# Convolution, LayerNorm sums, q/k norms and scores re-arranged in one step of a hybrid attention and convolution encoder

## The chip, the cores and the metric

The kernel runs on one core of one Trainium2 chip. TensorE (PE) multiplies matrices; VectorE (DVE), ScalarE (ACT) and GpSimd (POOL) do elementwise work; SyncE (SP) issues DMAs. PSUM is the memory into which TensorE accumulates, SBUF the working memory, HBM the memory outside. The metric is the device time of one launch in microseconds (us), smaller being better. Every engine takes its instructions in a fixed order.

## The reference

One layer for 1024 prompt frames and 32 sample frames of 1024 channels, 16 heads of 64. Cut to what matters:

```python
h = rmsnorm(x, norm_g)
q = rmsnorm(cols(OFF_Q), q_g) * HEAD_DIM ** -0.5      # per head
k = rmsnorm(cols(OFF_K), k_g)                         # cols(a) = h @ w_in[:, a:a + w]
v = cols(OFF_V);  logf = log_sigmoid(cols(OFF_F) + b_f)
u = cols(OFF_UA) * sigmoid(cols(OFF_UB))
ga, gb, ma, mb = cols(...), ...
s = einsum('bqhd,bkhd->bhqk', q, k) + C[t] - C[s]     # C = cumsum(logf), causal
o = softmax(s) @ v
conv = causal_dwconv(u_ext, w_dw) + b_dw              # width 31, per channel
ya = (o * silu(ga)) @ w_pa
yb = (silu(layernorm(conv, ln_g, ln_b)) * silu(gb)) @ w_pb
y = x + (sigmoid(ma) * ya + sigmoid(mb) * yb) @ w_out
```

The 32 sample frames attend to 512 cached keys besides their own, and their convolution starts from 30 cached rows. q, k, v, log f and the last rows of u are outputs too. Everything is float32 with a small tolerance, so a product is built of three: each operand is split into a high part of reduced precision and the rest, and TensorE multiplies high by high, rest by high and high by rest.

## The kernel before, in words

Prompt and sample stand side by side as 1056 columns. A projection of 128 output channels (`steps`, L102) takes 24 matmuls for each of three chunks of 352 columns; each chunk is accumulated in one PSUM bank and then evacuated. Its weights are loaded as `raw`, cast to the high part `wh` by ScalarE (L85) and split into the rest `wl` by GpSimd (L88). In the first half of the program five PSUM banks are handed round for such chunks.

The stages, in program order:

1. **Input.** A run of idle matmuls (L253), then tokens are normalised (`x_norm`), transposed by TensorE and split (`x_split`), in four column chunks; the first convolution input u0 (from the groups "ub" and "ua") is projected along with them, with a sigmoid for each chunk.
2. **u1 and v.** `u_proj(1)` makes the next 128 channels of u. Then v is projected token-major in four column groups of 260 (256 of v, 4 of f), nine row tiles each (eight prompt tiles of 128 rows and one sample tile of 32). u2 stands between the second and the third group.
3. **log f, q and k.** The log-sigmoid is computed by an exp and a series of short DVE operations at high priority (L408 to L423). Then 8 times "k" and "q": each chunk is squared by ScalarE, split, summed over the 64 channels of a head by TensorE (`bones`, L476 and L477), and turned into 1/root by a Sqrt on ScalarE (L479) and a reciprocal on VectorE (L480); L481 multiplies. u3 stands at f = 3.
4. **Gates ga**, with u4, u5, u6 between them.
5. **Attention.** 16 heads of 8 query blocks. A block's `scores` go into one of two PSUM buffers `psS`; VectorE takes the maximum (L659), ScalarE the exp (L661) into one of three buffers `P`, VectorE 1/sum (L663), GpSimd scales (L664). `turn` transposes P on TensorE (L681) and splits it (L685, L686); `values` multiplies by v (L697, L698). Between the parts of a block, `fill(4)` runs four steps of three matmuls of an unrelated projection: u7 and 21 gate tiles. The sample's four groups of heads stand among the blocks.
6. **Last stage.** The 3 gate tiles left over, then the projections "pa", "pb" and "out", with `ln_out` making the convolution branch's input beside "pa".

The convolution is done by VectorE: per 128 channels 30 `tap`s (L168), each a multiply-add over 1086 columns, after a first tap on ScalarE (L166). The taps of u(f) are put into a list, and `pump` takes some of them out between the pieces of other work, from stage 2 into the attention. The finished y(f) is added to `mean` (L172, L174) and stored. LayerNorm then works inside the attention: mean over channels by TensorE, y loaded again, mean subtracted (L742), stored, squared, squares summed by GpSimd (L747), 1/root (L756, L757), y loaded a third time, multiplied (L763) and stored.

What sets the order: a scheduler lays out every engine's instructions at build time by its own estimate of times and by priorities (evacuations stand high, taps low); only TensorE's order in the attention is as written. On the chip an engine waits at the head of its order whatever stands behind it.

## Time and profile before

| | |
|---|---|
| time, median of 3 runs | 1467.45 us (1467.08 to 1468.04) |
| the profiled execution | 1474.0 us, its span 1472.2 us |
| mean granted TensorE clock | 0.982 |
| TensorE busy | 1422.8 us, 97% of the span |
| VectorE, ScalarE, GpSimd busy | 943.6, 627.4, 690.8 us |
| DMA | 217.47 MB, 148 GB/s over the span |

TensorE's busy time counts pipelined matmuls, so an engine that is busy all the time may still issue less than it could. It is read together with the number of matmuls in a stretch and the granted clock: a stretch of pure 352-column projections without a stall holds 159 matmuls in 25 us. The profiled execution took 6.55 us more than the median of the runs. By time the stages lie so: input to 54 us, u1 and v to about 214, q and k to about 450, ga to about 616, attention to about 1160, last stage to 1472.

### The profile page before, as it was taken

Reading aid. Unit: us, or ns where it says so; the run is one execution under the profiler, and the core shown is the slowest. Engines: PE = TensorE matmul, PEld = TensorE weight load, DVE = VectorE, ACT = ScalarE, POOL = GpSimd, SP = SyncE. Lnnn points to the kernel's source line nnn. Section 1 sums busy time; section 2 is a strip of 40 time slices with the busy share of each in tenths; the row PEclk is TensorE's granted clock in tenths of the full one; section 3 lists DMA queues with packets and bytes.
Section 4 is the critical chain, followed back from the end, with each engine's and each line's share of the span. In section 5 each row is a group of like instructions: output and inputs, shape, how many; then the busy total and the mean of one; then the engine's idle time right before and its main releaser. Section 6 shows DMA issues by size and latency. Waiting matters only on the chain.

```text
span 1472.2 us, 24868 instructions
## 1 busy us (share of the span) xinstructions
PE 1422.8 (97%) x9465; PEld 1379.1 (94%) x9465; DVE 943.6 (64%) x1194; ACT 627.4 (43%) x1257; POOL 690.8 (47%) x734
## 2 busy tenths in 40 slices
PE   8999898999999999899999999899999999999999
PEld 7899898999999999898899999788999999999998
DVE  5699898849995999979955545765554442132211
ACT  6423124444554222264455555664555486222110
POOL 3488444747885343444534334634332364244321
PEclk9999999999999999999999999999999999999999
DMA  4244233333455522243555456857552597444421
GB/s 172 76 139 153 81 139 114 120 120 106 144 174 165 158 96 90 79 116 103 136 171 148 140 155 189 284 176 258 175 155 69 194 337 265 145 129 155 146 88 50
DMA packets 114935, 217.47 MB, mean 148 GB/s; under 512 B 17856, under 2 KB 75072, under 8 KB 114816
## 3 DMA queue, kind: packets, MB, share of 16 engines
q1 hardware_dynamic: 114384, 215.52, 46.5%
q8 instruction: 75, 1.23, 0.4%
q14 instruction: 44, 0.36, 0.1%
q10 hardware_dynamic: 432, 0.37, 0.1%
HBM read 137.89 MB, written 77.95 MB: 147 GB/s over the span
## 4 chain that ended last, share of the span: by engine, by line
PE 60%; DVE 12%; DMA 3%; ACT 2%; issue 1%; POOL 1%; SPq 0%; DVEq 0%; ACTq 0%
PE pj L96 46%; DVE y L168 10%; PE ptr L681 4%; PE po L697 2%; PE po L698 2%; PE psS L654 2%; PE psS L655 2%; DMA yv<-s_y 1%; DMA V<-s_v 1%; DVE ri L480 1%; DMA s_y<-yv 1%; PE po L605 1%; DVE yv L742 1%; PE psS L657 0%; POOL wl L88 0%
## 5 line engine op out<-in xcount | busy, mean ns | idle before, releaser
L96 PE MATMUL pj<-xh,wh 128*128 128x352 f32 (+2 forms) x1552 | 514.9, 333 | 9.2 <-DVE qn L481 3.2
L96 PE MATMUL pj<-xh,wl 128*128 128x352 f32 (+2 forms) x1552 | 500.4, 323 | 1.1 <-POOL wl L88 1.1
L96 PE MATMUL pj<-xl,wh 128*128 128x352 f32 (+2 forms) x1552 | 499.7, 325 | 0.0
L88 POOL TENSOR_TENSOR wl<-raw,wh 128x384 fp32r<-128x384 f32 (+1 forms) x264 | 306.4, 1190 | 323.2 <-ACT wh L85 318.7
L168 DVE SCALAR_TENSOR_TENSOR y<-u,vec_t,y 128x1086 f32<-128x1086 f32 x240 | 378.6, 1577 | 24.1 <-ACT y L166 14.8
L96 PEld LDWEIGHTS pj<-xh,wh 128*128 128x128 f32 x1552 | 295.7, 191 | 13.4 <-ACT xh L325 4.7
L96 PEld LDWEIGHTS pj<-xh,wl 128*128 128x128 f32 x1552 | 296.7, 191 | 2.3 <-POOL wl L88 2.3
L96 PEld LDWEIGHTS pj<-xl,wh 128*128 128x128 f32 x1552 | 293.6, 191 | 0.3
L664 POOL TENSOR_SCALAR P<-P,nm 128x128 f32<-128x128 f32 (+7 forms) x128 | 111.4, 871 | 234.2 <-DVE nm L663 219.0
L85 ACT CAST wh<-raw 128x1024 fp32r<-128x1024 f32 x88 | 92.2, 1048 | 159.5 <-PE pj L96 123.5
L659 DVE TENSOR_REDUCE nm<-psS 128x1 f32<-128x128 f32 (+7 forms) x128 | 96.4, 753 | 72.3 <-PE psS L657 56.6
L685 ACT CAST pth<-ptr 128x512 fp32r<-128x512 f32 (+1 forms) x192 | 86.9, 481 | 97.7 <-PE ptr L681 96.6
L480 DVE RECIPROCAL ri<-ri 128x352 f32<-128x352 f32 x48 | 112.0, 2339 | 23.4 <-ACT ri L479 23.3
L686 DVE TENSOR_TENSOR ptl<-ptr,pth 128x512 fp32r<-128x512 f32 (+1 forms) x192 | 101.9, 550 | 18.1 <-ACT pth L685 16.0
L661 ACT ACTIVATE P<-psS,nm 128x128 f32<-128x128 f32 (+7 forms) x128 | 95.3, 744 | 39.3 <-DVE nm L659 32.8
L681 PE MATMUL ptr<-ident,P 128*128 128x128 f32 x576 | 86.8, 278 | 14.2 <-POOL P L664 11.5
L382 PE MATMUL pjv<-vwh,xh 128*128 128x260 f32 (+1 forms) x288 | 82.3, 286 | 4.6 <-DVE u L212 4.6
L382 PE MATMUL pjv<-vwl,xh 128*128 128x260 f32 (+1 forms) x288 | 82.2, 285 | 0.0
L382 PE MATMUL pjv<-vwh,xl 128*128 128x260 f32 (+1 forms) x288 | 82.2, 285 | 0.0
L697 PE MATMUL po<-pth,V 128*128 128x256 f32 x320 | 79.3, 284 | 1.7 <-DMA V<-s_v 1.7
L698 PE MATMUL po<-ptl,V 128*128 128x256 f32 x320 | 78.3, 282 | 0.0
L681 PEld LDWEIGHTS ptr<-ident,P 128*128 128x128 f32 x576 | 62.9, 143 | 15.9 <-POOL P L664 12.2
(188 smaller groups left out, 2530.8 us busy)
## 6 DMA issues: line engine op xcount, KB each, us to landing
raw<-wf SPq DMA_DIRECT2D x88, 512.0 KB
yv<-s_y SPq DMA_DIRECT2D x16, 528.0 KB
s_y<-yv SPq DMA_DIRECT2D x16, 528.0 KB
s_v<-vb SPq DMA_DIRECT2D x32, 256.0 KB
QB<-s_q SPq DMA_DIRECT2D x32, 256.0 KB
KB<-s_k SPq DMA_DIRECT2D x32, 256.0 KB
V<-s_v SPq DMA_DIRECT2D x16, 512.0 KB
kT<-qn SPq DMA_DIRECT2D x8, 528.0 KB
```

The lines of the kernel that those rows point to most:

```text
L88: nc.gpsimd.tensor_sub(wl[:, k0:k1, :], raw[:, k0:k1, :], f32(wh[:, k0:k1, :]))
L96: nc.tensor.matmul(ps, a[:, kt, :], b(kt, sl), start=(first and n == 0), stop=(last and n == N - 1))
L168: nc.vector.scalar_tensor_tensor(ys[0], u[:, i:i + CW], w, ys[0], op0=ALU.mult, op1=ALU.add)
L382: nc.tensor.matmul(ps[:r, :VC], a, b, start=(n == 0), stop=(n == 23))
L480: nc.vector.reciprocal(ri, ri)
L659: nc.vector.tensor_reduce(nm[:, 0:1], ps[:, :nb, :w], axis=AX.XY, op=ALU.max, negate=True)
L661: nc.scalar.activation(P[:, :nk].rearrange("p (b w) -> p b w", b=nb), ps[:, :nb, :w], AF.Exp, bias=nm[:, 0:1], accum_out=nm[:, 1:2])
L664: nc.gpsimd.tensor_scalar(P[:, :nk], P[:, :nk], nm[:, 2:3], 1.0, op0=ALU.mult, op1=ALU.mult)
L681: nc.tensor.transpose(pt[:, 128 * j:128 * j + 128], P[:, 128 * (4 * u + j):128 * (4 * u + j) + 128], ident)
L686: nc.vector.tensor_sub(ptl[:, js, qo], p3, f32(pth[:, js, qo]))
L697: nc.tensor.matmul(po[:, :256], V[:, j, :], pth[:, j, :], start=(j == 0), stop=False)
L698: nc.tensor.matmul(po[:, :256], V[:, j, :], ptl[:, j, :], start=False, stop=(j == njb - 1))
```

## The change

**Convolution.** u3 now stands ahead of q and k, u4, u5, u6 at f = 2, 4, 6 and u7 ahead of the ga gates, so all eight convolutions are issued before the attention, and their pool is closed before it. There are two y buffers instead of one. The attention's fills are 22 gate tiles, without u7; 2 gate tiles are left for the last stage, and two blocks of head 8 have no fill.

**LayerNorm.** `conv_done` stores y(f) and then works on it while it lies in SBUF: it subtracts a shift, the mean over the first 128 channels of y(0) (four float32 matmuls, `shift_of`), adds the rest to `mean` (DVE), squares it in place (ACT) and adds the squares to `rstd` (POOL). In the attention only the two sums over channels remain, the variance is their difference, and 1/root is made by Ln and Exp. `ln_out` subtracts the mean and multiplies by 1/root itself (two DVE operations per tile), so y is loaded once and not stored again.

**Norms by log and exp.** In `x_norm` and in q and k the root and its reciprocal become Ln and Exp on ScalarE, from one preloaded table; after each u's sigmoid the table is loaded again. The log-sigmoid moves behind f = 1, without high priority.

**Scores.** Scores are issued three blocks ahead of their turn instead of two; the loads of heads and samples one block earlier. The number of psS and P buffers stays.

**v.** A group's sample tile (24 matmuls) becomes 8 float32 matmuls, four of which write to different 32-row groups of one bank; the four partial sums are added by ScalarE and VectorE.

**Input.** Three column chunks instead of four, some squares on VectorE, u0's sigmoid once at the end, 46 idle matmuls instead of 56.

Three places where the order moved. First VectorE ahead of the evacuation of u2 (its multiplication by the sigmoid, L212 before and L248 now). Before, from the last evacuation of u1:

```order
L168 SCALAR_TENSOR_TENSOR y<-u,vec_t,y 128x1086 x16
L172 COPY mean<-y 128x1024
L172 COPY mean<-y 128x32
L168 SCALAR_TENSOR_TENSOR y<-u,vec_t,y 128x1086 x25
L212 TENSOR_TENSOR u<-pj,u 128x352
```

Now the end of the same piece (taps are L212 here; 6 of them stand ahead of the first row):

```order
L212 SCALAR_TENSOR_TENSOR y<-u,vec_t,y 128x1086 x13
L437 TENSOR_REDUCE vs<-v_1099 32x260
L212 SCALAR_TENSOR_TENSOR y<-u,vec_t,y 128x1086 x2
L438 COPY z<-vs 32x4
L212 SCALAR_TENSOR_TENSOR y<-u,vec_t,y 128x1086 x14
L189 TENSOR_TENSOR y<-y,shift 128x1024
L189 TENSOR_TENSOR y<-y,shift 128x32
L212 SCALAR_TENSOR_TENSOR y<-u,vec_t,y 128x1086
L192 COPY mean<-y 128x1024
L192 COPY mean<-y 128x32
L212 SCALAR_TENSOR_TENSOR y<-u,vec_t,y 128x1086 x7
L248 TENSOR_TENSOR u<-pj,u 128x352
```

From the start of the convolution to u2's evacuation there were 55 taps and are 57 now, and two reductions for the sample's v and the subtraction of the shift have come in.

Second ScalarE where v ends. Before, q and k begin there (L472, L473), behind the exp of the log-sigmoid:

```order
L386 COPY vf<-pjv 32x256
L390 COPY z<-pjv 32x4
L413 ACT_TABLE_LOAD
L413 ACTIVATE ee<-az 128x144
L472 ACTIVATE sqf<-pj 128x352
L473 CAST sqh<-sqf 128x352
```

Now u3 stands there (L241 are the copies of its "ub" chunks), and the exp, the square of a finished convolution (L195) and the cast of k's first weights (L91) stand among them:

```order
L241 COPY u<-pj 128x352
L478 ACT_TABLE_LOAD
L478 ACTIVATE ee<-az 128x144
L241 COPY u<-pj 128x352
L195 ACTIVATE y<-y 128x1086
L241 COPY u<-pj 128x320
L241 COPY u<-pj 128x32
L91 CAST wh<-raw 128x1024
L244 ACT_TABLE_LOAD
L244 ACTIVATE u<-u 128x1024
L244 ACTIVATE u<-u 128x32
L564 ACT_TABLE_LOAD
```

k's first weights now stand behind the square, which itself stands behind VectorE's subtraction and sum.

Third TensorE at the first `turn` of the attention. Before (psS are scores, ptr the transposes, pj the fills):

```order
L96 MATMUL pj<-xl,wh 128x352
L654 MATMUL psS<-KB,QB 128x384
L655 MATMUL psS<-KA,QA 128x384
L657 LDWEIGHTS identb
L657 MATMUL psS<-cmaskb,identb 128x128
L681 MATMUL ptr_6485<-ident,P 128x128
```

Now:

```order
L102 MATMUL pj<-xl,wh 128x352
L731 MATMUL psS<-KB,QB 128x384
L732 MATMUL psS<-KA,QA 128x384
L734 LDWEIGHTS identb
L734 MATMUL psS<-cmaskb,identb 128x128
L731 MATMUL psS<-KB,QB 128x512
L732 MATMUL psS<-KA,QA 128x512
L734 LDWEIGHTS identb
L734 MATMUL psS<-cmaskb,identb 128x128
L758 MATMUL ptr_6595<-ident,P 128x128
```

The scores of the fourth block have moved ahead of the first block's transposes.

The diff, cut to its core:

```diff
-LNO = ((0, 1), (2, 3), (4, 5), (6, 7), (), (), ())
-NFILL = 21
-NWARM = 56
+LNO = ((0,), (1, 2), (3,), (4, 5), (6,), (7,), ())
+LNEXP = "natural_log_exp_and_others"
+NFILL = 22
+NGA = 8
+NWARM = 46
-XCH = ((0, 256), (256, 256), (512, 256), (768, 288))
+XCH = ((0, 256), (256, 384), (640, 416))
...
+    def shift_of(y):
+        shift = cvp.tile([128, TT], F32, name="shift", bufs=1)
+        ones = cvp.tile([128, 128], F32, name="ones", bufs=1)
+        nc.vector.memset(ones, 1.0)
+        with tc.high_priority(offset=3000):
+            for c in range(3):
+                pm = st.tile([128, 512], F32, name="psh", tag="st")
+                for a, b in pieces(c * CH, CH):
+                    o = slice(b.start - 30, b.stop - 30)
+                    nc.tensor.matmul(pm[:, a], ones, y[:, o], start=True, stop=True)
+                nc.scalar.mul(shift[:, csl(c)], pm[:, :CH], 1.0 / 128)
+        nc.sync.dma_start(s_m, shift)
+        return shift
+
+    def conv_done(f, y):
+        nc.sync.dma_start(s_y[f, :, :T], y[:, :T])
+        nc.sync.dma_start(s_y[f, :, T:], y[:, T + 30:])
+        if f == 0:
+            sides["shift"] = shift_of(y)
+        shift = sides["shift"]
+        for o, n, a in PCS:
+            nc.vector.tensor_sub(y[:, o:o + n], y[:, o:o + n], shift[:, a:a + n])
+        for o, n, a in PCS:
...
+                nc.vector.tensor_add(mean[:, a:a + n], mean[:, a:a + n], y[:, o:o + n])
+        nc.scalar.activation(y, y, AF.Square)
...
+                nc.gpsimd.tensor_add(rstd[:, a:a + n], rstd[:, a:a + n], y[:, o:o + n])
...
-                ys.append(cvp.tile([128, CW], F32, name="y", tag="y", bufs=1))
+                ys.append(cvp.tile([128, CW], F32, name="y", tag="y"))
...
-                        nc.scalar.activation(u[:, b], pss[0][:, a], AF.Sigmoid)
-                    for a, b in pieces(o, n):
-                        nc.vector.tensor_mul(u[:, b], pss[1][:, a], u[:, b])
+                        nc.scalar.copy(u[:, b], pss[0][:, a])
+                    nc.vector.tensor_copy(ua0[:, sl], pss[1][:, :n])
+                    if c == 2:
+                        for o2, n2, a2 in PCS:
+                            b = slice(30 + o2, 30 + o2 + n2)
+                            nc.scalar.activation(u[:, b], u[:, b], AF.Sigmoid)
+                            nc.vector.tensor_mul(u[:, b], ua0[:, a2:a2 + n2], u[:, b])
...
+        ps = pj.tile([128, 512], F32, name="pjs", tag="pj")
+        for n in range(2):
+            for j in range(4):
+                nc.tensor.matmul(ps[32 * j:32 * j + 32, :VC], xsm[:, 2 * j + n, :], raws2[j // 2][:, (2 * j + n) % 4, :],
+                                 start=(n == 0), stop=(n == 1))
...
-            nc.scalar.activation(ri, pm[:, :CH], AF.Sqrt, bias=eps_t, scale=1.0 / HD)
-            nc.vector.reciprocal(ri, ri)
+            with tc.issue_after(sides["tables"].ins):
+                nc.scalar.activation(ri, pm[:, :CH], AF.Ln, bias=eps_t, scale=1.0 / HD)
+                nc.scalar.activation(ri, ri, AF.Exp, scale=-0.5)
...
+    u_proj(3, pj, n=1)
+    tables_again()
     for f in range(8):
-        if f == 3:
-            u_proj(3, pj, n=1)
+        if f in (2, 4, 6):
+            u_proj(3 + f // 2, pj, n=1)
+            tables_again()
         qk("k", f)
         qk("q", f)
         if f == 1:
+            log_sigmoid()
+        if f == 2:
             forget_sums()
...
-        if n in (0, 2, 4):
-            u_proj(4 + n // 2, pj, n=3)
-        for whole in gate_steps(g, f, pj):
+    u_proj(7, pj, n=2)
+    for f in range(NGA):
+        for whole in gate_steps("ga", f, pj):
             if whole:
-                pump(3)
+                pump(2)
+    pump(len(taps))
+    pcv.close()
...
-        if n + 2 < len(seq):
-            start(seq[n + 2])
+        if n + 3 < len(seq):
+            start(seq[n + 3])
...
+        nc.vector.tensor_sub(y, y, mean)
+        nc.vector.tensor_mul(y, y, rstd)
         nc.scalar.activation(y, y, AF.Silu, bias=vcol(V_LNB, f), scale=vcol(V_LNG, f))
```

195 lines of the change are left out of this document (101 added, 94 removed).

## Prediction

> **What bounds the kernel now.** I read the busy times first, then the stages, the waits of TensorE, and the chain that ended last.
>
> ```profile
> PE 1422.8 (97%) x9465; PEld 1379.1 (94%) x9465; DVE 943.6 (64%) x1194; ACT 627.4 (43%) x1257; POOL 690.8 (47%) x734
> ...
> PE pj L96 46%; DVE y L168 10%; PE ptr L681 4%; PE po L697 2%; PE po L698 2%; PE psS L654 2%; PE psS L655 2%; DMA yv<-s_y 1%; DMA V<-s_v 1%; DVE ri L480 1%; DMA s_y<-yv 1%; PE po L605 1%; DVE yv L742 1%; PE psS L657 0%; POOL wl L88 0%
> ```
>
> TensorE sets the end, yet 10% of the chain is convolution taps: somewhere VectorE is what TensorE waits for. The stages tell where matmuls are lost:
>
> ```profile
> core 0: us, PE busy (x) PEld busy (x) DVE busy (x) ACT busy (x) POOL busy (x), PEclk, DMA share, GB/s
> 214.00:300.00 86.00, 76.68 (x461) 75.45 (x460) 71.19 (x68) 36.54 (x73) 46.58 (x50) 0.94 0.37 115
> 300.00:600.00 300.00, 299.43 (x1875) 299.03 (x1875) 255.85 (x191) 115.87 (x210) 175.60 (x161) 1.00 0.42 129
> 620.00:760.00 140.00, 129.76 (x875) 120.86 (x874) 116.62 (x189) 71.03 (x160) 62.82 (x79) 0.94 0.46 129
> 760.00:900.00 140.00, 139.26 (x997) 130.58 (x996) 73.06 (x161) 74.98 (x173) 50.05 (x94) 1.00 0.51 146
> 900.00:1050.00 150.00, 138.92 (x934) 128.10 (x933) 97.20 (x167) 85.33 (x178) 66.11 (x88) 0.95 0.74 233
> 1050.00:1152.00 102.00, 101.76 (x740) 95.76 (x739) 53.71 (x118) 54.53 (x125) 35.95 (x66) 1.00 0.39 113
> 1152.00:1472.20 320.20, 316.69 (x2000) 316.40 (x1998) 81.99 (x126) 104.56 (x134) 120.51 (x110) 1.00 0.51 171
> ```
>
> From 300 to 600 us 1875 matmuls take 300 us: .160 us each, so 24 of them 3.84 us and a u projection (six times 24) 23 us. In the attention the stretch 760 to 900 issues 997 in 140 us, 7.12 per us. At that rate 875 take 122.9 us, so 620 to 760 loses 17.1; 934 take 131.2, so 900 to 1050 loses 18.8; 1050 to 1152 loses nothing. The attention loses 36 us, and exactly where VectorE also has the taps of u7 (116.62 us busy), or has the LayerNorm passes and the DMA is at .74. From 214 to 300, 461 matmuls at .160 would take 73.8: 12.2 lost. The waits name what is late:
>
> ```profile
> PE ptr L681 <- POOL P L664: 11.5, 5, 3.0
> PE pst L476 <- ACT sqh L473: 6.6, 1, 6.6
> PE pjv L382 <- DVE u L212: 4.6, 1, 4.6
> PE pj L96 <- DVE qn L481: 3.2, 2, 2.7
> ACT ee L413 <- DVE az L412: 11.7, 1, 11.7
> PE psS L654 <- ACT P L661: 2.3, 1, 2.3
> ```
>
> Three are VectorE's doing: u2's product behind taps; sqh, which stood behind an exp that waited 11.7 us for VectorE; qn behind the reciprocals. The first is GpSimd's, inside the attention:
>
> ```profile
> 678.55 4.36 POOL L88 TENSOR_TENSOR wl<-raw,wh 128x384 fp32r<-128x384 f32 x3
> 682.89 2.76 POOL L664 TENSOR_SCALAR P<-P,nm 128x1024 f32<-128x1024 f32 x2
> 684.33 1.09 PE L681 MATMUL ptr<-ident,P 128*128 128x128 f32 x8 [2.86 <-POOL P L664]
> ...
> 675.00:700.00 25.00, 22.14 (x148) 21.26 (x147) 22.76 (x37) 11.18 (x27) 11.16 (x15) 0.93 0.45 122
> ```
>
> A block's scaling stands behind a 4.36 us weight split, its transposes come 2.86 us late, and TensorE then runs some time at a lower clock (.93 over these 25 us): a stall costs its wait and a slower stretch behind it.
>
> **Part 1, start to k's first weights: VectorE is the bound.** The input chunks, the fewer idle matmuls and the sample's v all shorten TensorE's work. A sample tile takes 24 matmuls, at
>
> ```profile
> 100.00:125.00 25.00, 25.00 (x211) 24.76 (x211) 21.70 (x15) 9.00 (x29) 20.98 (x15) 1.00 0.62 211
> ...
> 707.17 1.08 PE L570 MATMUL psS<-kc,qs_t 64*32 64x512 f32 x8
> ```
>
> .118 us each (25/211): 2.8 us per group. Eight matmuls of a small operand over 512 columns take 1.08 us in the attention; the new ones are of 260 columns, but full float32, so between .5 and 2.1 us. I take 1.7: 1 us per group saved, 4 in all (the bounds give 3 to 9). The input I put at 5 us less (0 to 8: ten idle matmuls and one of four chunk passes fewer). But TensorE already waited 4.6 us for VectorE at u2, and VectorE gets more to do:
>
> ```profile
> core 0: us, DVE busy (x), PEclk, DMA share, GB/s
> 58.00:166.00 108.00, 99.59 (x56) 0.99 0.37 120
> 166.00:226.00 60.00, 52.64 (x35) 0.96 0.37 126
> ...
> 165.23 0.52 DVE L212 TENSOR_TENSOR u<-pj,u 128x352 f32<-128x352 f32 x1
> ...
> DVE y L168 <- ACT y L166: 2.9, 1, 2.9
> ...
> 675.78 1.22 DVE L659 TENSOR_REDUCE nm<-psS 128x1 f32<-128x1024 f32 x1
> ...
> L742 DVE TENSOR_TENSOR yv<-yv,mean 128x1056 f32<-128x1056 f32 x8 | 13.5, 1697 | 5.5 <-DMA yv<-s_y 5.3
> L174 DVE TENSOR_TENSOR mean<-mean,y 128x1024 f32<-128x1024 f32 x7 | 10.1, 1440 | 0.1
> ```
>
> A tap takes 1.78 us up to 166 us (99.59/56), 1.50 after. Before, u2's product came at 165.2. Ahead of it now stand two more taps (3.6), two reductions over 1040 values (1.2 each by the maximum's row, 2.4), and the subtraction of the shift (1.4 to 1.7 for 1024 columns by the rows of L174 and L742, and .5 for the sample's 32: 2.2). That is 8.2 more. Less are 2.9, the wait of the second convolution's first tap for the only y buffer, and about 2, which the convolution starts earlier (the 5 us less one whole sigmoid, its table and product): u2's product at **168**, 166 to 171. TensorE is there at 160.6 (165.2 less the 4.6) less 5 and 2, 153.6 or earlier: it waits about 14 us, in place of 4.6, and all its savings go into that wait.
>
> From there TensorE needs 49.3 us (165.2 to 214.5, where v ended before) less 2 for v, and 23 for u3, which now follows: k could start at 238. But k's first weights wait for VectorE too:
>
> ```profile
> 228.77 1.03 DVE L415 RECIPROCAL ac<-ac 128x144 f32<-128x144 f32 x1
> 229.84 1.01 DVE L416 TENSOR_TENSOR ee<-ee,ac 128x144 f32<-128x144 f32 x1
> ...
> L85 ACT CAST wh<-raw 128x1024 fp32r<-128x1024 f32 x88 | 92.2, 1048 | 159.5 <-PE pj L96 123.5
> L747 POOL TENSOR_TENSOR rstd<-rstd,sqv 128x1056 f32<-128x1056 f32 x7 | 17.2, 2464 | 4.4 <-ACT sqv L746 4.4
> L88 POOL TENSOR_TENSOR wl<-raw,wh 128x384 fp32r<-128x384 f32 x176 | 210.3, 1217 | 323.2 <-ACT wh L85 318.7 <-DMA raw<-wf 4.3
> ...
> 228.84 0.66 PE L476 MATMUL pst<-sqh,bones 128*128 128x352 f32 x1 [6.64 <-ACT sqh L473]
> ```
>
> From 168 VectorE has 33 taps of 1.50 (49.5), two convolutions' ends (subtraction 2.2, sum 1.9 each: 8.2), two reductions (2.4), the rest of u2's products (1.3), and the log-sigmoid's operations ahead of the last sum (two of 1 us, five short ones and the wait for exp: 5): 234.5. Behind that sum ScalarE squares y (1.3, as many columns as a tap), and GpSimd adds the squares (2.5, and .5 for the sample) before it makes the rest of k's weights (1.2); ScalarE's cast (1.05) lies beside the sum. k starts at **240**, 236 to 245, TensorE waiting a second time for 2 us. Before, the same point is 214.5, plus 23 for u3, plus the stall at 228.84 with the slower clock behind it, 8.3 (6.64 and a quarter of it): 245.8. Part 1 gives **-6**, between -10 and 0.
>
> *By the skill.* Two taps with GpSimd quiet show what a tap costs alone:
>
> ```profile
> 165.66 2.73 DVE L168 SCALAR_TENSOR_TENSOR y<-u,vec_t,y 128x1086 f32<-128x1086 f32 x2
> 55.00:120.00 65.00, 63.49 (x473) 62.09 (x474) 57.97 (x36) 20.02 (x45) 56.03 (x33) 1.00 0.42 135
> ```
>
> They took 1.37 us each against 1.78 with GpSimd busy 86% of the time. The Trainium skill, page "SBUF — State Buffer", section "SBUF: two separate sides", says that a VectorE operation with two SBUF inputs and a GpSimd operation that reads SBUF exclude each other for a whole instruction. A tap is such an operation, and the rows agree in direction. By that rule a tap that always finds a 1.2 us split half done would wait .6 × .86 and take 1.9: 57 taps would be 7 us later, and the time 1433.5 instead of the 1426.5 below. The sum goes by the measured 1.78.
>
> **Part 2, q and k.**
>
> ```profile
> L480 DVE RECIPROCAL ri<-ri 128x352 f32<-128x352 f32 x48 | 112.0, 2339 | 23.4 <-ACT ri L479 23.3
> ```
>
> 112 us of VectorE are removed, 48 times 2.34; ScalarE gets one more pass over 352 columns per chunk (a third of the cast's 1.05), and has 115.87 of 300 us in use. TensorE does not wait from 300 to 600, so only the stall for qn near 289 is gone: of the 12.2 lost from 214 to 300, 8.3 are counted in part 1, **-4** remain. The taps now come at 30 per two f: 45 us of taps, 12 products of a third of a tap (6) and one convolution's end (4.1), 55 us, against 73 of TensorE (six chunks' worth of u and 12 of q or k, 4.16 each with their sums): VectorE keeps up, and its late taps are gone before the attention. Each u's table is loaded twice more; the chunk behind it can be late by an us or so: **+1** (0 to 4). u4 to u7 are moved, not changed: 0, since TensorE is full in either place. Their moved loads and stores lie in a stage where the DMA share is .42.
>
> **Part 3, attention.** u7's taps, products and 16 stores and loads of y leave it, with the second and third LayerNorm pass. VectorE falls from 116.62 and 97.20 to near the 73.06 of the clean stretch, and GpSimd loses the 17.2 us of L747. Scores a block earlier give each scaling one block more. I take the clean stretch as what all of it comes to, with two heads' worth of stalls left (4 us, the table loads of the new logarithm among them): **-32**, between -36 and -10, the latter if the splits in front of the scalings (678.55), which remain, are the cause. The 22 gate tiles hold as many fills as before; u7 moved out, and one tile fewer is left over: equal work. ln_out's two operations per tile (1.7 and 1.4) lie in a last stage where VectorE has 82 of 320 us in use: 0.
>
> **Sum.** The profiled execution took 1474.0: -6 -4 +1 -32 makes 1433. It was 6.55 above the median of the runs, 1467.45; the same off gives **1426.5**.
>
> **The rivals.**
>
> *Early savings come through.* If taps run near 1.37 in part 1, VectorE is 57 × .41 = 23 us earlier and TensorE is the bound: 5 and 4 saved, the u2 wait gone with its slow stretch (6), the 8.3 gone, table load and sigmoid back (3): -20 instead of -6, **1412.5**. For it speaks the quiet pair; against it that GpSimd has the same splits there. Chance .2.
>
> *Half of the attention's loss stays.* Only the u7 part (17.1) goes, since the other stretch has the DMA at .74, and new Ln and Exp follow Silu with a table to load each, in the order of the engine that owes the exps: 15 us more, **1441.5**. For it: L664's wait is GpSimd's, and its splits remain. Chance .17.
>
> *Scores wait in front of their turn: slower.* There are still two score buffers. The scores of block n+3 need block n+1's exp, and now stand ahead of block n's transposes. If that exp is not done, TensorE stands, with transposes, fills and values queued behind it.
>
> ```profile
> L661 ACT ACTIVATE P<-psS,nm 128x128 f32<-128x128 f32 (+7 forms) x128 | 95.3, 744 | 39.3 <-DVE nm L659 32.8
> ```
>
> A wait of one exp and its sum (.744 and .2) in each of the 64 larger of 128 blocks is 60 us, so +28 instead of -32: **1486.5**. It decides once maximum and exp come later than one block's span, 3.9 us (540 us of attention less 36, over 128 blocks). Before, this wait was 2.3 us once, and ScalarE has 74.98 of 140 us in use: chance .08.
>
> **Chances.** The forecast has .55, its own range 1415 to 1438. With the rivals on both sides the range is 1402 to 1451; outside lie the slower case and the tails. About .2%, 3 us, is what a measurement can tell from no change: faster .91, same .02, slower .07.
>
> **What would show it.** Right: u2's product near 168 with a TensorE wait of 10 us or more for it; k's first chunk near 240; no waits for sqh or qn; over 7 matmuls per us in every stretch of the attention, and no wait of psS for P above 5 us in sum. Wrong: u2's product before 160 (first rival); ptr still waiting for P some 10 us (second); psS waiting for P tens of times (third). VectorE not through with taps when the ga gates end would undo part 2, since the attention waits for that pool.

## The result, and the profile after

The changed kernel takes 1516.01 us (median of 4 runs, 1504.53 to 1518.14) where the kernel before takes 1467.54: a ratio of 1.0319, 95% interval 1.0273 to 1.0364. It is 3.2% slower. I had forecast 1426.5, and 1402 to 1451 as the range.

The profiled execution is the shortest of the four, 1504.5 us, with a span of 1502.7. First its page: busy times, then the lines of the chain that ended last.

```profile
PE 1427.2 (95%) x9383; PEld 1377.0 (92%) x9383; DVE 892.5 (59%) x1154; ACT 664.0 (44%) x1316; POOL 748.5 (50%) x743
...
PE pj L102 39%; PE ptr L758 4%; PE po L774 2%; PE po L775 2%; PE psS L731 2%; PE psS L732 2%; DMA kc<-ckT 1%; POOL wl L94 1%; DMA raw<-wf 1%; PE po L682 1%; PE psS L734 1%; DMA QA<-s_q 1%; DMA KA<-s_k 0%; POOL sql L539 0%; DVE y L907 0%
```

VectorE is 51 us less busy, though 112 us of reciprocals are gone, and its taps have left the chain. GpSimd is 58 us busier, though the change gave it no work that it had not before (the sums of the convolution's squares took 17 us before and take 20 now, 3 of them for the sample's columns). The waits of TensorE name it:

```profile
PE pst L542 <- POOL sql L539: 33.5, 23, 3.3
PE psh L176 <- DVE y L212: 11.6, 1, 11.6
PE psS L731 <- ACT P L738: 3.7, 1, 3.7
...
POOL rstd L200 <- ACT y L195: 27.5, 6, 9.1
```

To see where the time went, I cut both executions at five points: the first and the last sum over a head's channels (L476 before, L541 now), the attention's first score, its last product, the last matmul. Projections that the change moved from one stretch to another are moved in the figures of before too: 23 us for each u, 11.5 for a gate tile.

| from, to | before, with the moved projections | after | difference | forecast |
|---|---|---|---|---|
| start, first sum in q/k | 228.8 + 23 = 251.8 | 252.3 | +0.5 | -6 |
| first, last sum in q/k | 227.9 - 23 + 69 = 273.9 | 319.0 | +45.1 | -3 |
| last sum, attention | 159.5 - 69 + 23 = 113.5 | 111.1 | -2.4 | 0 |
| attention | 543.4 - 11.5 = 531.9 | 513.2 | -18.7 | -32 |
| last stage | 309.1 - 11.5 = 297.6 | 303.7 | +6.1 | 0 |
| sum | 1468.7 | 1499.3 | +30.6 | -41 |

The loss is q and k, where I had put a gain. Their stretch in the table by stretch, and VectorE's taps in the same stretch, before (229 to 457 us) and after (252 to 571):

```profile
229.00:457.00 228.00, 224.76 (x1383) 223.41 (x1384) 192.35 (x153) 108.04 (x216) 162.87 (x163) 0.99 0.41 134
229.00:457.00 228.00, 44.57 (x30) 0.99 0.41 134
```

```profile
252.00:571.30 319.30, 285.54 (x1669) 277.61 (x1670) 254.02 (x201) 151.29 (x289) 267.15 (x185) 0.96 0.32 108
252.00:571.00 319.00, 208.26 (x120) 0.96 0.32 108
```

Before, VectorE passed 30 taps through q and k, and most of its time there went to the reciprocals. Now it passes 120. That is four convolutions' worth, those of u3 to u6: the change put the projections of u4, u5 and u6 into q and k, and their taps came along, out of the ga stage. I had counted them (30 per two f) and had set them against VectorE's time alone. And GpSimd is busy 84% of the stretch instead of 71%, with the same kinds of instructions, because each takes longer:

```profile
L474 POOL TENSOR_TENSOR sql<-sqf,sqh 128x352 fp32r<-128x352 f32 x48 | 50.1, 1045 | 8.9 <-ACT sqh L473 8.9
```

```profile
L539 POOL TENSOR_TENSOR sql<-sqf,sqh 128x352 fp32r<-128x352 f32 x48 | 82.8, 1732 | 5.9 <-ACT sqh L538 5.8
L553 POOL TENSOR_TENSOR ql<-qn,qh 128x352 fp32r<-128x352 f32 x32 | 54.1, 1697 | 0.0
```

The first row is of before, the others of after: a split of the same 352 columns takes 1.73 us instead of 1.05. The timeline of the two engines, side by side at one wait, shows four taps and what GpSimd does meanwhile:

```profile
351.78 7.16 DVE L212 SCALAR_TENSOR_TENSOR y<-u,vec_t,y 128x1086 f32<-128x1086 f32 x4
...
351.92 2.01 POOL L553 TENSOR_TENSOR ql<-qn,qh 128x352 fp32r<-128x352 f32 x1
353.89 3.90 POOL L539 TENSOR_TENSOR sql<-sqf,sqh 128x352 fp32r<-128x352 f32 x2
357.75 1.99 POOL L553 TENSOR_TENSOR ql<-qn,qh 128x352 fp32r<-128x352 f32 x1
...
355.91 0.43 PE L542 MATMUL pst<-sql,bones 128*128 128x352 f32 x1 [1.74 <-POOL sql L539]
```

Singly, the taps begin at 351.78, 353.16, 355.11 and 357.04 us and the splits at 351.92, 353.89, 355.82 and 357.75: after the first, one of each per 1.94 us. The two engines go in step, and TensorE waits for the split.

### The profile page after: what moved, and what is told of

Read it like the earlier page. It is cut to its first block, busy times and chain, and to the rows that moved or that the text cites. A ratio compares the mean times of both kernels' runs of the same rounds, so it can differ in the third digit from the quotient of the medians.

```text
span 1502.7 us, 24731 instructions
## 1 busy us (share of the span) xinstructions
PE 1427.2 (95%) x9383; PEld 1377.0 (92%) x9383; DVE 892.5 (59%) x1154; ACT 664.0 (44%) x1316; POOL 748.5 (50%) x743
## 4 chain that ended last, share of the span: by engine, by line
PE 54%; DMA 3%; ACT 2%; POOL 1%; DVE 1%; issue 1%; SPq 1%; ACTq 0%; POOLq 0%
PE pj L102 39%; PE ptr L758 4%; PE po L774 2%; PE po L775 2%; PE psS L731 2%; PE psS L732 2%; DMA kc<-ckT 1%; POOL wl L94 1%; DMA raw<-wf 1%; PE po L682 1%; PE psS L734 1%; DMA QA<-s_q 1%; DMA KA<-s_k 0%; POOL sql L539 0%; DVE y L907 0%
## 5 line engine op out<-in xcount | busy, mean ns | idle before, releaser
L94 POOL TENSOR_TENSOR wl<-raw,wh 128x384 fp32r<-128x384 f32 (+1 forms) x258 | 308.9, 1224 | 286.6 <-ACT wh L91 268.4
L212 DVE SCALAR_TENSOR_TENSOR y<-u,vec_t,y 128x1086 f32<-128x1086 f32 x240 | 409.6, 1714 | 18.2 <-ACT y L210 12.4
L741 POOL TENSOR_SCALAR P<-P,nm 128x128 f32<-128x128 f32 (+7 forms) x128 | 95.6, 747 | 262.1 <-DVE nm L740 211.9
L91 ACT CAST wh<-raw 128x1024 fp32r<-128x1024 f32 x86 | 90.2, 1048 | 152.2 <-PE pj L102 109.8
L539 POOL TENSOR_TENSOR sql<-sqf,sqh 128x352 fp32r<-128x352 f32 x48 | 82.8, 1732 | 5.9 <-ACT sqh L538 5.8
L449 PE MATMUL pjv<-vwh,xh 128*128 128x260 f32 x256 | 73.8, 288 | 5.0 <-ACT z L456 5.0
L449 PE MATMUL pjv<-vwh,xl 128*128 128x260 f32 x256 | 73.9, 289 | 0.0
L449 PE MATMUL pjv<-vwl,xh 128*128 128x260 f32 x256 | 73.3, 286 | 0.0
L731 PE MATMUL psS<-KB,QB 128*128 128x256 f32 (+2 forms) x192 | 68.8, 360 | 4.3 <-ACT P L738 3.7
```

The lines of the kernel that those rows point to most:

```text
L94: nc.gpsimd.tensor_sub(wl[:, k0:k1, :], raw[:, k0:k1, :], f32(wh[:, k0:k1, :]))
L212: nc.vector.scalar_tensor_tensor(ys[0], u[:, i:i + CW], w, ys[0], op0=ALU.mult, op1=ALU.add)
L449: nc.tensor.matmul(ps[:, :VC], a, b, start=(n == 0), stop=(n == 23))
L731: nc.tensor.matmul(ps[:, b, :wm], QB[:, qsl], KB[:, ksl], start=True, stop=False)
L741: nc.gpsimd.tensor_scalar(P[:, :nk], P[:, :nk], nm[:, 2:3], 1.0, op0=ALU.mult, op1=ALU.mult)
```

## The experiments

Three theories for q and k. **L**: VectorE instructions with two operands in SBUF (a tap reads u and y) and GpSimd's splits take turns at SBUF; reciprocals read one operand and had left GpSimd free. **H**: GpSimd's new additions (L200) stand at the head of its queue until ScalarE has squared, 27.5 us in all, and hold up the splits behind them. **A**: ScalarE is late, with Ln, Exp and their tables.

### One-operand instructions in place of the taps

```diff
+            if f in (2, 3, 4, 5) and i < KC - 1:
+                nc.vector.reciprocal(ys[0][:, i:i + 210], u[:, i + 31:i + 241])
+            else:
                 nc.vector.scalar_tensor_tensor(ys[0], u[:, i:i + CW], w, ys[0], op0=ALU.mult, op1=ALU.add)
```

> The changed kernel with 29 of the 30 VectorE taps of the convolutions 2 to 5 replaced by reciprocals over 210 columns, about as long (1.4 us) but with one SBUF operand; the convolution branch is wrong by that. VectorE is as busy as before, by count and by time. Theory L: sql near 1.0 us, TensorE's wait for it under 5 us in sum, and 35 to 45 us less: 1465 to 1482. Theories H and A: VectorE's operands don't matter, the wait stays 25 to 35 us, 1500 to 1520.

This kernel leaves out most of four convolutions. Measured: 1467.03 us, ratio to the kernel before .9994 (.9970 to 1.0018), 49 us less than the changed kernel. VectorE's 116 stand-ins took 1.46 us each, more than a tap alone (1.38, measured below), so a lighter VectorE is not the reason; sql fell to 1.22 us over all and TensorE's wait for it to 7.8 us, both a little above what L had put, with the taps of one convolution, u6's, left in q and k. The time fits L; H and A forecast no change.

### Without the convolution's squares

```diff
+        if f in (2, 3, 4, 5, 6):
+            return
         nc.scalar.activation(y, y, AF.Square)
```

> The changed kernel without the square and the sum of squares of the convolutions 2 to 6 (ScalarE's pass and GpSimd's two additions), so the variance of the LayerNorm lacks them. Theory H: the 27 us in which GpSimd stood with its addition at the head of its queue, and with them most of TensorE's waits for sql, go: 1475 to 1490. Theory L: only 5 of some 150 turns of GpSimd go, 2.7 us each: sql stays above 1.6 us and 0 to 10 us are gained, 1495 to 1516. Theory A: five ScalarE passes of 1.1 us, 0 to 5 us.

Measured: 1514.09 us (ratio 1.0305, 1.0280 to 1.0330). The split of the squares took 1.73 us as before and TensorE waited 34.5 us for it. H falls: an engine that stands idle at its queue's head was not what the others waited for.

### Without the low part of the squares

```diff
-            nc.scalar.activation(sqf, ps, AF.Square)
-            nc.scalar.copy(sqh, sqf)
-            nc.gpsimd.tensor_sub(sql, sqf, f32(sqh))
+            nc.scalar.activation(sqh, ps, AF.Square)
...
-            nc.tensor.matmul(pm[:, :CH], bones, sqh, start=True, stop=False)
-            nc.tensor.matmul(pm[:, :CH], bones, sql, start=False, stop=True)
+            nc.tensor.matmul(pm[:, :CH], bones, sqh, start=True, stop=True)
```

> The changed kernel without the low part of the squares in q and k: ScalarE writes the squares in reduced precision at once, GpSimd's split and one of the two sums per chunk are left out. TensorE has 48 x .16 = 7.7 us less to do, GpSimd 48 splits less, ScalarE 48 casts less. Theory L: with a third of GpSimd's turns in q and k gone, the two engines no longer fill the port; the stalls of 42 us go almost wholly, 1460 to 1480. Theory H: the other splits (ql, wl) still stand behind the waiting addition, and the loss moves to waits for wl: 1490 to 1505. Theory A: 48 casts of .48 us less on ScalarE, the stalls halved: 1480 to 1495.

Measured: 1475.78 us (ratio 1.0045, 1.0022 to 1.0067), 40 us less than the changed kernel, as L had it; some 8 of them are the 48 sums that TensorE no longer makes (.16 us each). The stretch of q and k took 276 us, near the 273.9 of before. That 13.0 us of waits for ScalarE's square are left gives A a small part. Alone this run cannot tell L from a GpSimd that is merely overloaded; the one with one-operand instructions can.

### The reciprocal back

```diff
-            with tc.issue_after(sides["tables"].ins):
-                nc.scalar.activation(ri, pm[:, :CH], AF.Ln, bias=eps_t, scale=1.0 / HD)
-                nc.scalar.activation(ri, ri, AF.Exp, scale=-0.5)
+            nc.scalar.activation(ri, pm[:, :CH], AF.Sqrt, bias=eps_t, scale=1.0 / HD)
+            nc.vector.reciprocal(ri, ri)
```

> The changed kernel with the Sqrt on ScalarE and the reciprocal on VectorE back in q and k, nothing else undone. Theory L (turns at the port): in q and k VectorE's taps, which read two SBUF operands, and GpSimd's splits take turns, about 1.97 us for a tap and a split together; the reciprocals read one operand and gave GpSimd free runs. Then the split of the squares (sql) falls from 1.73 us to about 1.1, TensorE's wait for it from 33.5 us to under 10, and the stretch from the first to the last sum over a head's channels (322 us) to about 290; some of it comes back as taps that end later, so 1470 to 1500 us in all. Theory H (head of GpSimd's queue: the sum of squares of the convolution waits there for ScalarE, and the splits behind it): sql stays at 1.7 us, the wait stays near 30, 1500 to 1520. Theory A (ScalarE is late because of Ln, Exp and their tables): the wait falls, but sql keeps its 1.7 us.

Measured: 1518.27 us (ratio 1.0350, 1.0312 to 1.0388). The number lies in the range of H, but neither of its signs came; L had 1470 to 1500. sql fell to 1.38 us and the wait for it to 14.4, in L's direction and short of its numbers; the stretch of q and k took 317 us. What the split gave back, VectorE took, as TensorE's waits in that stretch show:

```profile
PE pj L102 <- DVE qn L546: 14.8, 8, 3.4
PE pst L542 <- POOL sql L539: 14.4, 6, 3.2
PE pst L542 <- POOL u L226: 1.9, 1, 1.9
```

VectorE is busy for 312 of the 317 us: 103 taps take 166 us of them and 46 reciprocals 107. The taps are in q and k with the reciprocals as without them, and the stretch is about as long either way, first by VectorE and GpSimd together, here by VectorE alone. So the experiment fails as a proof of L, and it shows that the missing reciprocals are not what the loss needs: the taps that were moved into q and k are. What the reciprocals' removal alone would do, with the taps left where they were, was not tried.

### The price by itself

Behind the changed kernel's last output I put stretches in which both engines start together (four stretches, 12 splits each, with 16 instructions of VectorE beside them), and one in which each runs alone.

```diff
+    def split():
+        nc.gpsimd.tensor_sub(pl, pw, f32(ph))
...
+    for op, n in ((tap_s, 16), (rec, 16), (tap_p, 16), (tap_s, 16)):
+        for i in range(n):
+            op(i)
+        for _ in range(12):
+            split()
+        meet(pp if op is tap_p else py)
```

> The changed kernel with a measurement behind its last output, in stretches that begin together: 12 taps alone, 12 GpSimd splits (128x384) alone, then 12 splits beside 16 taps from SBUF, beside 16 reciprocals over 210 columns, beside 16 taps that accumulate in PSUM (1024 columns), and beside 16 taps from SBUF once more. Theory L: alone a tap takes 1.1 to 1.4 us and a split about 0.95; beside taps from SBUF either both stretch to about 2 us each, in turns, or one engine's instruction waits through many of the other's (a split of 10 us and more); beside reciprocals and beside taps in PSUM the split keeps 0.95 to 1.1 us and the other its own pace. Without a lock (a share of bandwidth, or a slower GpSimd in q and k for another reason) all four stretches show the same split time within a fifth.

Measured once, 1665.99 us with the added stretches; what counts are the durations inside. The timeline of VectorE (L1012 taps in SBUF, L1018 reciprocals, L1015 taps that accumulate in PSUM), then of GpSimd (all L1021); the first taps and the first splits are each alone:

```profile
1524.81 16.60 DVE L1012 SCALAR_TENSOR_TENSOR py<-pu,gt,py 128x1086 f32<-128x1086 f32 x12 [0.41 <-ACT pu L1027]
...
1555.41 29.39 DVE L1012 SCALAR_TENSOR_TENSOR py<-pu,gt,py 128x1086 f32<-128x1086 f32 x16 [0.64 <-ACT pu L1027]
...
1585.41 23.97 DVE L1018 RECIPROCAL pr<-pu 128x210 f32<-128x210 f32 x16 [0.43 <-ACT pu L1027]
...
1610.13 21.16 DVE L1015 SCALAR_TENSOR_TENSOR pp<-pu,gt,pp 128x1024 f32<-128x1024 f32 x16 [0.43 <-ACT pu L1027]
...
1541.76 12.76 POOL L1021 TENSOR_TENSOR pl<-pw,ph 128x384 fp32r<-128x384 f32 x12 [17.61 <-ACT pw L1033]
1555.15 22.96 POOL L1021 TENSOR_TENSOR pl<-pw,ph 128x384 fp32r<-128x384 f32 x12 [0.63 <-ACT pw L1026]
1585.37 12.77 POOL L1021 TENSOR_TENSOR pl<-pw,ph 128x384 fp32r<-128x384 f32 x12 [7.26 <-ACT pw L1026]
1610.09 12.80 POOL L1021 TENSOR_TENSOR pl<-pw,ph 128x384 fp32r<-128x384 f32 x12 [11.96 <-ACT pw L1026]
```

Alone a tap takes 1.38 us (16.60/12) and a split 1.06 (12.76/12). Beside taps from SBUF a split takes 1.91 (22.96/12), and so, nearly, does a tap. Beside reciprocals, and beside taps whose accumulator lies in PSUM, a split takes 1.06 and 1.07, as alone, and VectorE keeps its own 1.50 and 1.32. The repeat beside taps gave 22.96 again. This is L, with its price: a tap and a split together take 1.91 us. That a tap also writes SBUF is not the reason: in the changed kernel qn's product (L547) reads one operand from SBUF, one from PSUM and writes SBUF, and all 48 took .57 to .59 us, nearly all of them beside GpSimd.

By it q and k can be estimated. 120 taps and 185 GpSimd instructions stand in 319 us. If they met wholly, 120 pairs would take 229 us and the other 65 splits 69, 298 of 319: VectorE and GpSimd together fill most of the stretch, while TensorE's work takes 267 (the next run).

### The same everywhere

```diff
+            if i < KC - 1:
+                nc.vector.reciprocal(ys[0][:, i:i + 210], u[:, i + 31:i + 241])
+            else:
                 nc.vector.scalar_tensor_tensor(ys[0], u[:, i:i + CW], w, ys[0], op0=ALU.mult, op1=ALU.add)
```

> The changed kernel with 29 of the 30 VectorE taps of all eight convolutions replaced by reciprocals over 210 columns, as long, with one SBUF operand (the convolution branch is wrong by that). Against the run that did this for the convolutions 2 to 5 alone (1467 us): if the port also sets the first 240 us, no GpSimd split takes over 5 us there, TensorE's waits for the shift, for u2 and for v's banks fall from some 25 us to under 8, and the time is 1435 to 1452. If VectorE's mere load sets it, as I had forecast, the taps take as long as now and the time stays at 1460 to 1470.

This kernel leaves out most of every convolution. Measured: 1425.46 us (ratio .9709, .9684 to .9734), below the range that L had. The stretches of the table by it: 227.9, 267.3, 112.8, about 507 and 305 us. Against the changed kernel's first profile the start gives 24 us and q and k 52. The stretch of q and k here, to be read against the row 252.00:571.30:

```profile
228.00:495.00 267.00, 267.00 (x1670) 266.43 (x1669) 216.61 (x198) 150.04 (x288) 161.73 (x182) 1.00 0.37 126
```

The same 1670 matmuls without any gap, 182 of the 185 GpSimd instructions in 161.73 us instead of 267.15. The stand-ins took 1.46 us, again more than a tap alone. So the turns cost the start of the program too, where I had seen VectorE as the bound and taken its taps as given: their 1.78 us contained the splits.

### The changed kernel again

> The changed kernel unchanged, for its spread: its first profile took 1504.5 us, its other runs 1515 to 1518. Three profiles of kernels that keep its first 150 us show a single GpSimd split of v's weights that took 20.9 us, under 15 taps back to back, and TensorE waiting 16.3 us behind it; its own profile shows none. Theory L (turns at the port): the two engines fall by chance into turns (a tap and a split in 1.97 us together) or into runs of taps that keep GpSimd out, and the spread is this: a profile of 1512 us or more has a split above 10 us in the first 150 us, one of 1506 or less has none. If a long profile has none, the 12 us lie elsewhere.

Measured: 1511.42 us (1508.57 to 1516.56; ratio 1.0297, 1.0264 to 1.0330), its profile 1510.6. This profile lies between the two bounds that I had set, so the expectation isn't decided as it was put. It does show a long split, in GpSimd's timeline and then VectorE's:

```profile
88.71 23.24 POOL L422 TENSOR_TENSOR vwl<-vraw,vwh 128x520 fp32r<-128x520 f32 x2
...
94.36 16.45 DVE L212 SCALAR_TENSOR_TENSOR y<-u,vec_t,y 128x1086 f32<-128x1086 f32 x13
```

Two splits took 23.24 us, the second of them 20.9, while 15 taps ran past it at 1.27 us (16.45/13), no slower than alone in the stretch by itself (1.38). Here the engines do not alternate: the split ends at 111.95 us, 1.1 us after the last of these taps. Behind it ScalarE's copies of v wait, and TensorE 16.3 us for their banks. In the first profile there is no such split, and TensorE waits 11.6 us for the shift's operand instead. The first sum in q and k came at 258.1 us here and at 252.3 there, 6 us that are part of the spread. What decides between turns and a run of taps I haven't found.

### Scores two ahead

```diff
-    start(seq[2])
...
-        if n + 3 < len(seq):
-            start(seq[n + 3])
+        if n + 2 < len(seq):
+            start(seq[n + 2])
```

> The changed kernel with scores two blocks ahead again instead of three, the rest kept. The attention takes 514 us in the changed kernel, 544 before with one more projection tile in it (11.5 us): 18 us were won where I had forecast 32. If the third block is what won them, transposes wait some 10 us for GpSimd's scaling again and the time is 10 to 20 us longer, 1520 to 1535. If the moved taps and LayerNorm passes won them, the time stays within 5 us of the changed kernel's. If the third block costs (scores in front of their turn), it is 5 us shorter or more.

Measured: 1517.18 us (ratio 1.0321, 1.0281 to 1.0362); its attention took 510.9 us against 512.5 and 513.2 in the two profiles of the changed kernel. The third block ahead won nothing and cost nothing: the waits for GpSimd's scaling (11.5 us before) do not come back without it. What is left of the change in the attention, the moved taps and LayerNorm passes, most likely took them away; I haven't tried these apart.

### The accumulator in PSUM

The stretch by itself shows a way out: a tap that accumulates in PSUM leaves GpSimd free.

```diff
-    pjA = pool("pjA", 4, stack=pps, space=PS)
+    pjA = pool("pjA", 3, stack=pps, space=PS)
...
-    st = pool("st", 2, stack=pps, space=PS)
+    st = pool("st", 1, stack=pps, space=PS)
+    yp = pool("yp", 1, stack=pps, space=PS)
...
-            nc.vector.scalar_tensor_tensor(ys[0], u[:, i:i + CW], w, ys[0], op0=ALU.mult, op1=ALU.add)
+            nc.vector.scalar_tensor_tensor(ys[0], u[:, i:i + T], w, ys[0], op0=ALU.mult, op1=ALU.add)
+            nc.vector.scalar_tensor_tensor(ys[1][:, T + 30:], u[:, T + 30 + i:CW + i], w, ys[1][:, T + 30:],
+                                           op0=ALU.mult, op1=ALU.add)
             if i == KC - 1:
-                conv_done(f, ys[0])
+                nc.scalar.copy(ys[1][:, :T], ys[0])
+                conv_done(f, ys[1])
```

> The changed kernel with the convolution's 1024 prompt columns accumulated in two PSUM banks in place of SBUF, the 32 sample columns in SBUF by a short second instruction per tap, ScalarE copying a finished convolution to SBUF; the projections' banks go from five to four, the small sums' from two to one. A tap then has one SBUF operand. Theory L: GpSimd's splits take 0.95 to 1.1 us throughout, no split above 5 us, the waits for sql under 8 us, at the price of 240 short instructions (.1 to .15 us, 24 to 36 us of VectorE's time): 1445 to 1475. If VectorE's load or the fewer banks bind, 1480 to 1520, with TensorE waiting for banks (ScalarE or VectorE as releaser of pj).

Measured: 1453.78 us (ratio .9907, .9876 to .9938): faster than both kernels, with everything computed.

```profile
L216 DVE SCALAR_TENSOR_TENSOR yps<-u,vec_t,yps 128x1024 f32<-128x1024 f32 x240 | 306.3, 1276 | 9.1 <-ACT yps L213 8.5
L217 DVE SCALAR_TENSOR_TENSOR y<-u,vec_t,y 128x32 f32<-128x32 f32 x240 | 100.8, 424 | 0.5
L546 POOL TENSOR_TENSOR sql<-sqf,sqh 128x352 fp32r<-128x352 f32 x48 | 45.7, 958 | 26.9 <-ACT sqh L545 26.9
...
PE pj L102 <- DVE qn L554: 11.0, 10, 4.5
```

A tap takes 1.28 us instead of 1.71 and a split .96 instead of 1.73; no split above 3.5 us is left, and no wait for sql. In q and k TensorE now waits for VectorE, 11.0 us. The short sample instruction costs .42 us in the mean, three times what I had put. Its median is .24 and its longest 2.35 us: it still reads two SBUF operands, and it shows the turn itself. VectorE, then GpSimd:

```profile
302.53 0.73 DVE L217 SCALAR_TENSOR_TENSOR y<-u,vec_t,y 128x32 f32<-128x32 f32 x1
...
302.27 0.94 POOL L560 TENSOR_TENSOR ql<-qn,qh 128x352 fp32r<-128x352 f32 x1 [1.40 <-DMA s_k<-ql]
```

The instruction ends at 303.26 us, .05 after the split. Between 241 and 331 us 21 of them stand apart in the timeline with over .3 us, and each ends .04 to .06 us after a GpSimd instruction that had begun ahead of it or with it: 32 columns wait until that is done. The tap of 1024 columns with its accumulator in PSUM took 1.19 to 1.29 us, all 240 of them.

Three variants followed. The first (shown against the kernel with two banks) moves one ga tile out of the stage ahead of the attention, so that three gate tiles are left for the last stage:

```diff
-NGA = 8
+NGA = 7
```

> The kernel with the convolution in PSUM (1453.8 us), one gate tile fewer ahead of the attention, so that three are left for the last stage as before the change. In all profiles of the changed kernel and its variants the last stage takes 304 to 305 us with two gates left, before 309 with three (11.5 us each): 6 us more than its work, with two waits of 2.0 us at the first matmuls of pa. If the third gate hid the attention output's way through HBM and its splits, 4 to 7 us less: 1447 to 1450. If not, no change (1452 to 1456).

Measured: 1459.75 us (ratio .9924, .9903 to .9944), by the medians 6 us slower than without it; neither range that I had given holds it. The last stage took 313.8 us with its third tile, 302.3 without the tile's 11.5, against 303.8, so 1.5 us were won; the attention took 519.9 us instead of 506.6, in the profiles of the longest run of this kernel and of the shortest of the other. A ga tile's evacuation is a Silu; with one of them in the attention the tables of the exps (L745) and of this evacuation (L596) are loaded 11 times instead of 5, 1.28 us each on ScalarE. I take them for the cause and have not tried them alone.

The second and the third accumulate all 1086 columns in three banks, one instruction per tap (again against the kernel with two banks, cut to the taps); the input's transposes use these three banks before, and one bank serves all small sums. The second has seven ga tiles ahead of the attention, the third eight:

```diff
-            nc.scalar.activation(ys[1][:, T + 30:], u[:, T + 30:CW], AF.Identity, bias=vcol(V_BDW, f), scale=w)
...
-            nc.vector.scalar_tensor_tensor(ys[0], u[:, i:i + T], w, ys[0], op0=ALU.mult, op1=ALU.add)
-            nc.vector.scalar_tensor_tensor(ys[1][:, T + 30:], u[:, T + 30 + i:CW + i], w, ys[1][:, T + 30:],
-                                           op0=ALU.mult, op1=ALU.add)
+            nc.vector.scalar_tensor_tensor(ys[0], u[:, i:i + CW], w, ys[0], op0=ALU.mult, op1=ALU.add)
```

> As the last, but the convolution accumulates all 1086 columns in three PSUM banks, in one instruction per tap, and the input's transposes use these banks before, with one bank for all small sums. The short sample instruction took .42 us, 100.8 us of VectorE's time in all; a tap of 1086 columns should take 1.33 us, 86 us less. If VectorE's lateness is what TensorE waits for in q and k and at the shift there (11.0 and 3.0 us, with the slower clock behind), 1432 to 1442; if the fewer banks at the input cost as much, 1445 to 1455.

> The convolution in three PSUM banks, one instruction per tap, with all eight ga tiles ahead of the attention again and two gate tiles for the last stage. With one ga tile in the attention its evacuations need another table than the exps (8 loads there instead of 5 by the two kernels with two banks), and the attention took 515 to 520 us instead of 507 with the same number of tiles. If that is the price: attention 505 to 510, last stage 304, 1438 to 1446 in all. If the two are a matter of when the attention starts, no change from 1453.

Measured: 1453.08 us (ratio .9879, .9858 to .9900) with seven, 1449.57 us (ratio .9863, .9841 to .9884) with eight. The first lies in the range that I had given for the case that the fewer banks cost as much as the short instruction, the second between its two cases. A tap took 1.35 us against an expected 1.33, the waits for qn fell to 2.0 us and less, and q and k to 281 us from 286.6; yet with eight ga tiles the first sum came at 241.5 us, as with two banks (241.2). The attention took 510.7 us with eight tiles ahead and 514.9 with seven, so the tables (the 8 loads in the expectation were miscounted, it is 11) are worth 4 us at most here; the two intervals overlap. The start stays at 241 us, where one-operand stand-ins reach 228, because of the input: of the windows up to 228 us, with three banks and eight tiles and then with the stand-ins,

```profile
0.00:54.00 54.00, 43.91 (x227) 35.24 (x228) 23.86 (x42) 22.06 (x43) 14.54 (x15) 0.94 0.35 127
54.00:80.00 26.00, 23.88 (x127) 21.41 (x127) 16.61 (x22) 11.44 (x17) 9.74 (x10) 0.93 0.27 83
...
0.00:54.00 54.00, 48.90 (x277) 44.19 (x278) 28.77 (x54) 27.63 (x53) 14.60 (x18) 0.94 0.34 127
54.00:80.00 26.00, 26.00 (x180) 25.18 (x180) 25.08 (x23) 10.88 (x17) 13.13 (x13) 0.99 0.43 129
```

the first two lack 103 matmuls by 80 us, and from there to 228 us both issue about the same (1161 and 1143). The input is where the banks were taken from; I have not tried that apart. The kernel with three banks and eight ga tiles is the fastest complete one, 1.4% faster than the kernel before.

## Why the prediction was wrong, point by point

**Part 1, start to k's first weights (-6; +0.5 to the first sum).** The end of this part held in the profiled execution, and not for the reason given. Two rows of the timeline, u2's product and k's second matmul:

```profile
161.49 0.51 DVE L248 TENSOR_TENSOR u<-pj,u 128x352 f32<-128x352 f32 x1
...
242.47 0.43 PE L102 MATMUL pj<-xh,wl 128*128 128x352 f32 x1 [2.03 <-POOL wl L94]
```

k began just ahead of a wait of 2.0 us for its weights that ended at 242.5 us, so at 240, as forecast. u2's product came at 161.5 us, not 168. TensorE did wait, 11.6 us, but for the shift's operand, the end of convolution 0, which I had not followed as a wait; other profiles have 16.3 us behind a split of v's weights. The rest of the -6 went behind k's start: before the first sum TensorE waits 2.0 us for the weights and 1.6 for the first square, and 1.7 us of the forecast's gain, the slower clock behind the old stall, lie behind that sum. The rival "early savings come through" named taps near 1.37 us as its condition and 1412.5 as its time; with the turns gone its time comes true (24 us at the start), by stand-ins of 1.46 us. I had set its chance at .2 with the words that GpSimd has the same splits there: that was the mechanism, read as an objection.

**Part 2, q and k (-3; +45.1).** This is the step that failed: "VectorE keeps up", a sum of VectorE's time in which GpSimd's splits stood at nothing. It set 55 us of VectorE for two f against 73 of TensorE, and never asked what GpSimd's splits cost once taps stand beside them. Taps went in at the measured 1.50, a mean over 166 to 226 us before, where GpSimd was busy 21.27 of 60 us (ahead of it, 88.00 of 108); in q and k they took 1.74 (208.26/120). Splits were not in the sum; their 1.05 us lay far under TensorE's 4.16 per chunk. But that 1.05 had been measured with 30 taps in the stretch, and the change put 120 there: a split of the squares took 1.73 us, and TensorE waited 33.5 us for it, with a slower clock behind (.96 over the stretch). Of the two steps that met in this part, the moved taps are the one that costs; with the reciprocals back the stretch was 317 us.

The rule that would have said so stood in the prediction, cited and used on one side alone. The Trainium skill, page "SBUF — State Buffer", section "SBUF: two separate sides", says that the two engines exclude each other whichever comes first; I worked out from it what VectorE's taps would lose (7 us) and not what GpSimd's splits would. The stretch by itself agrees with it in kind: 1.06 us beside one-operand instructions and beside a PSUM accumulator, 1.91 beside taps. It does not agree wholly in size, since a pair takes 1.91 us and not the 2.44 of the two alone.

**Part 3, attention (-32; -18.7).** The mechanism held: TensorE's waits for GpSimd's scaling fell from 11.5 us to none, and from 760 us to the end the attention issues 3125 matmuls in 435.6 us, 7.17 per us, the rate of the clean stretch. The size was off. My 36 us of loss began at 620 us, inside the attention's start, where TensorE issues little in either kernel (69 matmuls in the first 18 us before, 74 now); rows of after, the first from its first score:

```profile
682.00:700.00 18.00, 14.34 (x74) 12.73 (x75) 3.85 (x12) 7.11 (x16) 6.62 (x10) 0.81 0.32 94
740.00:760.00 20.00, 17.19 (x106) 15.45 (x105) 10.21 (x24) 18.00 (x33) 4.24 (x10) 0.91 0.39 94
```

74 matmuls in 18 us are 7.6 us under the rate of 7.12 per us, in a place that no moved work could fill, and the stretch with LayerNorm's sums over channels (740 to 760) is another 5. "Scores a block earlier" contributed nothing. The rival that kept half of the loss had the time of this part nearly right (15 us more than mine; 13.3 measured) and the wrong cause.

**The last stage (0; +6.1).** "Equal work" was right and the place was not: with two gate tiles in front instead of three, pa's first weights came late, two waits of 2.0 us, behind which matmuls stand .29 us apart for some 2.4 us instead of .16:

```profile
1277.91 0.43 PE L102 MATMUL pj<-ah,wh 128*128 128x352 f32 x1 [2.01 <-ACT wh L91]
1280.41 0.66 PE L102 MATMUL pj<-ah,wl 128*128 128x352 f32 x1 [2.07 <-POOL wl L94]
```

About 1.5 us of it went with a third tile (the variant with seven ga tiles); the rest stays open.

**The slower rival** (scores in front of their turn) did not happen: that wait was 3.7 us, once. I gave slower .07, all of it to this one. None of my rivals looked at an engine that gets slower by what another engine does beside it.

**The forecast's number.** 1426.5 was the time of a kernel in which the taps cost GpSimd nothing; the run that makes them so took 1425.5. That is partly chance: the start gave four times what I had put, the attention less.

## What to carry to other kernels

A duration in a profile belongs to what ran beside it: before instructions are moved, look what will stand beside them, and cost both engines' instructions by a row in which the new neighbour runs. Here the taps came out of a stage where TensorE had not waited and into one where it waits for GpSimd's splits; time that falls free on VectorE was no measure of what they cost there. Where VectorE's long instructions read two SBUF operands beside GpSimd's, try one accumulator in PSUM before counting either engine's idle time as free.

## What the runs showed of the hardware that I had not expected

- A tap and a GpSimd split beside each other take 1.91 us together, 1.38 and 1.06 alone; reciprocals with one SBUF operand, or taps with a PSUM accumulator, cost a split nothing (1.06 and 1.07).
- The turns are not kept: one split took 20.9 us while 15 taps passed it. It was seen in seven profiles of the changed kernel and its variants with taps in SBUF, and not in the first one of the changed kernel.
- An instruction of VectorE over 32 columns with two SBUF operands took .24 us in the median and up to 2.35: 21 of 21 long ones in a stretch of 90 us ended .04 to .06 us after the GpSimd instruction that they met. Instructions with one operand in PSUM kept their time beside the same splits (.57 to .59 us for qn's product).
